# The last gate's sums traced behind the first expert group's products, and that group's gather taken apart between them

## The chip, the cores and the metric

The kernel runs on one core of a Trainium2 chip. The metric is the device time of one execution in microseconds. An engine is named as the profile names it: PE is TensorE, DVE is VectorE, ACT is ScalarE, POOL is GpSimd, and SP is the engine whose queue issues nearly all loads.

## What is computed

Two decoder layers over 256 tokens of width 1024, each a mixer followed by a mixture of 16 experts, of which every token uses two. Each layer takes shift, scale and gate vectors from a conditioning vector c. Cut to what matters here:

```
for layer in range(2):
    shift_m, scale_m, gate_m, shift_f, scale_f, gate_f = split(silu(c) @ ada_w[layer] + ada_b[layer], 6)
    x = x + gate_m * mixer(rmsnorm(x) * (1 + scale_m) + shift_m)
    h = rmsnorm(x) * (1 + scale_f) + shift_f
    group, two experts, weights w = route(sigmoid(h @ router_w) + router_b)
    y = sum over the two experts: w_e * ((silu(h @ w_gate[e]) * (h @ w_up[e])) @ w_down[e])
    x = x + gate_f * y
return rmsnorm(x)
```

The last gate of a layer, gate_f (number 5 of the six vectors), multiplies the experts' rows at the very end of an expert group.

## The kernel before

All weights, 4 bytes an element, stream from HBM through 15 slots of 1 MB (ten tiles "slot" and five "room"). One queue, SP's, issues the loads in the order of use, and a load waits there until its slot is free; everything behind it waits too. The instructions of each engine are put in order by a planner: it takes at each moment, by its own costs, the ready instruction that was traced first (a block under high_priority(-60) counts as traced some 60 instructions later), and it fills idle time with anything that is ready.

An expert stage (function moe) runs so in each layer:

- Router: transposes and products of X (L989, L992), sigmoid, then a long chain of small DVE operations that picks two experts for each token and numbers each expert's tokens (M, pos, route).
- fill(12) at L1056, under high_priority(-60), makes the last gate. ada_part (L327) multiplies the 4 MB of its weights by silu(c) in two parts (L340: matmuls of 32 columns into a bank with the tag "tp"). The partial sums go to a tile "adac", copied by ACT (L347) and added by DVE (L349). ada_end (L301) then sums over partitions: for each half of the gate one product with HALF (L307) into a tp bank and one addition on DVE (L309) into GATE[5]. There are two tp banks and two adac tiles.
- picked and gather (L1199, L1067) bring the tokens of group 0 together. pick (L1064) makes one-hot rows, and for each of the eight 128-feature pieces k four matmuls (L1073) select tokens out of the normalized x, held as a high and a low part. ACT (L1075, odd k) or DVE (L1077, even k) then applies scale and shift on the way from the tp bank to XG.
- places (L1384) sorts 13 of the experts by their number of tokens, on DVE (L1393 to L1406, with two adac tiles). Its result ex_p (L1405) holds the sorted expert numbers, and SP must read it before it can issue the loads of experts that aren't fixed.
- Then the loop over seven groups of 128 gathered rows. hidden() issues a group's gate and up loads and runs gate_up (L1103): eight steps k of gate products and eight of up products (L1091), 16 steps in a row, each with two 64-column matmuls. slots() makes the matrices that bring rows back to tokens (by_slot, L1135 and L1137), turn() transposes the hidden values (L1125), and rows() of the group before runs its down products and multiplies by the gate (L1162). The gather for groups 1 and 2 follows group 0 and for groups 3 to 6 later ones.

Groups 0 and 1 are special in their weights: group 0 has the fixed experts 14 and 15, so its eight loads (L1192) are issued long before the routing, and of group 1 one expert is fixed, with three of its loads (L1254) also ahead. These 11 MB and the gate's 4 MB fill all 15 slots. Slots come free when L340 is through with the gate's weights, and after that only as the products of group 0 are done.

Of the kernel before, what the change touches and what calls it, by code (L numbers as in the profile page):

```python
# [107 lines left out]
def trunk(ctx, tc, ins, out):  # L108
# [192 lines left out]
    def ada_end(layer, v, n, t):  # L301


        if n == 1:
            for half in range(2):
                b = bank("tp", [P, 512])
                last[0] = mm(b, HALF[:, half:half + 1].to_broadcast([P, P]), t, start=True, stop=True)  # L307
                sl = slice(half * 512, half * 512 + 512)
                vec.tensor_tensor(GATE[v][:, sl], GATE[v][:, sl], b, ALU.add)  # L309
            return  # L310
        b = bank("tp", [64, 8, 4])
        for k in range(8):
            last[0] = mm(b[:, k, :], t[:, 64 * k:64 * k + 64], ident[:, 0:128:32], start=True, stop=True)
        for i in range(2):
            o = MOD[layer, v + i]
            for half in range(2):
                sl = slice(64 * half, 64 * half + 64)
                vec.tensor_tensor(o[sl], b[:, :, 2 * i + half], ADC[sl, layer, v + i, :], ALU.add)
            if i:
                vec.scalar_tensor_tensor(o, o, 1.0, NRM[:, (v // 3) * 2 + layer, :], ALU.add, ALU.mult)  # L320

    def ada_tile():
        return wk.tile([P, 512], F32, tag="adac", name="adac")

    fills, sums, last = [], [], [None]

    def ada_part(layer, v, n, j, W):  # L327


        if j == 0:  # L330
            if n == 1:
                GATE[v] = big.tile([P, D], F32, name="GATE", tag="GATE")
                pool.dma_start(GATE[v], ins["ada_b"][layer:layer + 1, v * D:(v + 1) * D].to_broadcast([P, D]))
            sums.append(ada_tile())
        t = sums[0]
        b = bank("tp", [P, 512])
        for i in range(2):
            for g in range(4):
                k = 2 * j + i if n == 2 else 4 * j + 2 * i + g // 2
                last[0] = mm(b[32 * g:32 * g + 32], csil[:, k, :], W[i][:, g, :], start=i == 0, stop=i == 1)  # L340
            if i == 0:
                yield
        o, i = t, b
        if n == 2:
            o, i = t.rearrange("p (k m) -> p m k", k=8), b.rearrange("p (m k) -> p m k", k=8)
        if j == 0:
            act.copy(o, i)  # L347
        else:
            vec.tensor_tensor(o, o, i, ALU.add)  # L349
        if j == 2 * n - 1:  # L350
            yield
            ada_end(layer, v, n, sums.pop())

    def fill(n=1):
        for _ in range(n):
            if fills:
                at = fills.pop(0)
                W = first.pop(0) if first else ada_load(*at)
                for _ in ada_part(*at, W):
                    pass  # L360
# [613 lines left out]
    def moe(cp, wk, layer, norm, end):  # L974
# [77 lines left out]
        vec.tensor_reduce(ws, Wt, AX.X, ALU.add)  # L1052
        vec.reciprocal(ws, ws)
        vec.tensor_tensor(Wt, Wt, ws.unsqueeze(2).to_broadcast([P, 2, 16]), ALU.mult)
        with tc.high_priority(-60):
            fill(12)  # L1056
        gate = GATE[5]

        def pick(o, at, m):
# [4 lines left out]
                vec.tensor_tensor(o[:, t].rearrange("p (e s) -> p e s", e=n), iota,  # L1064
                                  at[:, t].unsqueeze(2).to_broadcast([P, n, m]), ALU.is_equal)

        def gather(XG, n, o):  # L1067

            for k in range(8):
                b = bank("tp", [P, n])  # L1070
                for t in range(2):
                    for i in range(2):
                        mm(b, xk[i][:, t, k, :], o[:, t, 0:n], start=t == i == 0, stop=t == i == 1)  # L1073
                if k % 2:
                    act.activation(XG[:, k, :], b, AF.Identity, bias=sh[:, k:k + 1], scale=fa[:, k:k + 1])  # L1075
                else:
                    vec.tensor_scalar(XG[:, k, :], b, fa[:, k:k + 1], sh[:, k:k + 1], ALU.mult, ALU.add)  # L1077
# [22 lines left out]
            at = [a for a, n in enumerate(ns) for _ in range(n)]  # L1100
            return [(at[j], slice(BLOCK * j, BLOCK * j + BLOCK)) for j in reversed(range(4))]

        def gate_up(XG, c0, parts, Wg, Wu):  # L1103

            out = []
            for W, tag in ((Wg, "mm"), (Wu, "sc")):
                b = bank(tag, [P, 512])
                put = in_line()
                for k in range(8):
                    for a, at in parts:  # L1110
                        put(b[at], XG[:, k, c0 + at.start:c0 + at.stop], W[a][k], start=k == 0, stop=k == 7)
                out.append(b)
                flush()
            g, u = out
            hid = wk.tile([P, 512], F32, tag="hid", name="hid", bufs=1)
            hq = wk.tile([P, 512], F32, tag="hq", name="hq", bufs=1)
            act.activation(hid, g, AF.Silu)
            vec.tensor_tensor(by_k(hq, 4), features(u, 4), features(hid, 4), ALU.mult)  # L1118
            return hq
# [79 lines left out]
        def picked(groups, pos):  # L1199

            o = pick_tile()
            places, at = [x for g in groups for x in GROUPS[g]], 0
            while places:
                p0, m = places[0]
                n = 1
                while n < len(places) and places[n] == (p0 + n, m):
                    n += 1
                pick(o[:, :, at:at + n * m * BLOCK], pos[:, :, p0:p0 + n], m * BLOCK)
                at += n * m * BLOCK
                places = places[n:]  # L1210
            return o, at

        def gathered(o, n):
            XG = hp.tile([P, 8, n], F32, tag="HT", name="XG")
            gather(XG, n, o)
            return o, XG

        class Group:
# [19 lines left out]
            def hidden(self):  # L1238
                names = ("moe_w_gate", "moe_w_up")
                if self.first:  # L1240
                    W = [load_both(nm, self.p0) for nm in names]
                elif self.mixed:
                    W = self.load_mixed(*names)
                else:
                    W = [load_experts(nm, self.es, 8, fine=self.last and nm == names[1]) for nm in names]
                self.hid = gate_up(self.XG, self.c0, self.parts, *W)

            def load_mixed(self, gate_, up):

# [238 lines left out]
                        go(i + 1)  # L1488
            go(0)

        o, XG = gathered(*picked([0], route[:, 0:2]))
        places()
        for h in range(2):
            vec.tensor_scalar(OT_x[:, h], ident.unsqueeze(1).to_broadcast([P, 2, P]), 0.0, None, ALU.mult)
# [2 lines left out]
        for i in range(len(GROUPS)):  # L1497
            p = Group(i, o, XG, 128 * (i > 0 and i % 2 == 0))
            if i == 3:
                flush()  # L1500
                rest()
            if p.last:
                end.load()
            p.hidden()
            if before is not None:
                before.rows()
            p.slots()
            p.turn()
            if i % 2 == 0 and i < 5:
                o, XG = gathered(*then)  # L1510
            elif i < 5:
                then = picked([i + 2, i + 3], placed[:, 0:2])
            if i == 0:
                rounds()
            flush()
            before = p
# [296 lines left out]
```

## Time and profile before

| | |
|---|---|
| median of 3 runs | 831.33 us (828.41 to 831.84) |
| the profiled execution | 828.97 us, its span 827.3 us |
| PE busy | 730.9 us (88%) |
| DVE busy | 379.0 us (46%) |
| ACT busy | 233.7 us (28%) |
| mean transfer rate | 352 GB/s |

All times of the trace are microseconds from the start of the span. The busy share of PE is an average over stages with different limits, so the stages have to be looked at one by one. A matmul of fp32 is two instructions in the trace, and neighbours in different columns of the array run at the same time. PEclk is the TensorE clock that was granted, as a part of 2.4 GHz.

### The profile page before, as it was taken

What the parts mean: (1) busy time and instruction counts of PE and PEld (TensorE: products, weight loads), DVE (VectorE), ACT (ScalarE), POOL (GpSimd) and SP (SyncE); (2) the same over time, 40 slices, a digit from 0 to 9 for tenths busy, and PEclk for the clock granted to TensorE, in tenths of its full rate; (3) what the DMA queues carried; (4) which work ended last, traced back from release to release, by engine and by line L of the source; (5) the groups of instructions that cost most, each with busy time, mean ns of one, the idle gap of its engine ahead of it and who ended that gap; (6) DMA issues with size and microseconds to landing.
All of it is one profiled execution on the core that took longest, in us unless ns stands there. A gap on an engine that the chain in (4) does not pass through costs nothing. (4 is left out here: it accounts for less than half of the span.)

```text
span 827.3 us, 12080 instructions
## 1 busy us (share of the span) xinstructions
PE 730.9 (88%) x4435; PEld 376.0 (45%) x4435; DVE 379.0 (46%) x1099; ACT 233.7 (28%) x565; POOL 101.0 (12%) x94
## 2 busy tenths in 40 slices
PE   4599999999799997899887899969899988899886
PEld 2298765557433342234222568547443332233223
DVE  2585777777841240312305754885931230322214
ACT  2264555545411110001012455544310110011012
POOL 1020211132200000000001223353100000000001
PEclk9899999999799998999999999998799998999998
DMA  9999878598399999999999987747399999999992
GB/s 355 339 372 418 316 255 256 221 419 321 131 426 374 426 427 424 426 426 427 427 426 414 374 338 210 279 172 279 117 426 377 427 426 423 426 425 428 422 414 91
DMA packets 68457, 291.15 MB, mean 352 GB/s; under 512 B 9174, under 2 KB 23202, under 8 KB 42530
## 3 DMA queue, kind: packets, MB, share of 16 engines
q1 hardware_dynamic: 64048, 283.53, 86.0%
q0 software_dynamic: 1152, 4.21, 1.3%
q10 hardware_dynamic: 3186, 2.51, 0.9%
q8 instruction: 39, 0.64, 0.3%
q14 instruction: 32, 0.26, 0.1%
HBM read 289.16 MB, written 1.06 MB: 351 GB/s over the span
## 5 line engine op out<-in xcount | busy, mean ns | idle before, releaser
L1091 PE MATMUL mm<-slot,XG 128*32 128x512 f32 (+1 forms) x464 | 107.6, 643 | 12.3 <-DMA slot<-in_moe_w_down_dram 6.3
L1091 PE MATMUL o<-slot,hT 128*32 128x512 f32 (+2 forms) x480 | 88.6, 589 | 2.5 <-DMA slot<-in_moe_w_down_dram 2.5
L1118 DVE TENSOR_TENSOR hq<-sc,hid 128x512 f32<-128x512 f32 x14 | 14.7, 1049 | 151.5 <-PE sc L1091 151.5
L514 ACT CAST hl<-slot 128x512 fp32r<-128x512 f32 (+2 forms) x112 | 60.9, 557 | 72.3 <-PE mm L531 41.8
L471 POOL TENSOR_TENSOR hl<-slot,hl 128x512 fp32r<-128x512 f32 x40 | 52.8, 1323 | 158.8 <-ACT hl L514 145.2
L1091 PE MATMUL sc<-slot,XG 128*32 128x512 f32 (+1 forms) x344 | 72.1, 593 | 0.0
L1091 PE MATMUL sc<-room,XG 128*32 128x512 f32 (+1 forms) x296 | 60.7, 593 | 1.2 <-DMA room<-in_moe_w_up_dram 1.2
L1091 PEld LDWEIGHTS mm<-slot,XG 128*32 128x32 f32 (+1 forms) x464 | 27.7, 129 | 69.3 <-issue 67.3
L529 PE MATMUL mm<-HH,hl 128*128 128x256 f32 x176 | 54.2, 310 | 4.7 <-ACT HH L503 4.7
L1162 DVE SCALAR_TENSOR_TENSOR adac<-o,w,GATE 128x512 f32<-128x512 f32 (+1 forms) x29 | 21.2, 732 | 79.0 <-PE o L1091 77.7
L1144 ACT CAST yg<-adac 128x512 fp32r<-128x512 f32 (+1 forms) x28 | 17.1, 612 | 137.9 <-DVE adac L1162 137.9
L1091 PE MATMUL mm<-room,XG 128*32 128x512 f32 (+1 forms) x176 | 52.8, 678 | 0.0
L531 PE MATMUL mm<-HH,hl 128*128 128x256 f32 x176 | 50.0, 286 | 0.8 <-DVE hl L471 0.8
L530 PE MATMUL mm<-HH,hl 128*128 128x256 f32 x176 | 50.2, 287 | 0.0
L471 DVE TENSOR_TENSOR hl<-slot,hl 128x512 fp32r<-128x512 f32 (+2 forms) x72 | 43.3, 623 | 13.5 <-ACT hl L514 13.2
L1091 PE MATMUL o<-room,hT 128*64 128x512 f32 (+2 forms) x176 | 47.4, 577 | 2.2 <-DMA room<-in_moe_w_down_dram 2.0
L340 PE MATMUL tp<-slot,csil 128*32 128x512 f32 x344 | 45.5, 611 | 3.3 <-DMA slot<-in_ada_w_dram 3.1
L1151 PE MATMUL tp<-yg,OT 128*128 128x512 f32 (+1 forms) x112 | 38.1, 441 | 11.1 <-DVE X L1152 5.2
L1073 PE MATMUL tp<-pick,XH 128*128 128x256 f32 (+1 forms) x128 | 39.8, 333 | 8.1 <-DVE XG L1077 4.7
L1152 DVE TENSOR_TENSOR X<-X,tp 128x512 f32<-128x512 f32 (+1 forms) x56 | 36.1, 674 | 17.4 <-PE tp L1151 17.1
L1075 ACT ACTIVATE XG<-tp,mod,mod 128x256 f32<-128x256 f32 (+1 forms) x32 | 17.2, 538 | 94.9 <-PE tp L1073 94.9
L1091 PEld LDWEIGHTS o<-slot,hT 128*32 128x32 f32 (+1 forms) x480 | 24.9, 119 | 40.8 <-issue 34.2
(372 smaller groups left out, 1272.6 us busy)
## 6 DMA issues: line engine op xcount, KB each, us to landing
slot<-in_moe_w_gate_dram SPq DMA_DIRECT2D x48, 1024.0 KB, 13.4
slot<-in_ada_w_dram SPq DMA_DIRECT2D x43, 1024.0 KB, 10.2
slot<-in_moe_w_down_dram SPq DMA_DIRECT2D x42, 1024.0 KB, 19.4
slot<-in_moe_w_up_dram SPq DMA_DIRECT2D x35, 1024.0 KB, 14.4
room<-in_moe_w_up_dram SPq DMA_DIRECT2D x27, 1024.0 KB, 10.1
room<-in_moe_w_down_dram SPq DMA_DIRECT2D x18, 1024.0 KB, 15.3
room<-in_moe_w_gate_dram SPq DMA_DIRECT2D x16, 1024.0 KB, 12.2
slot<-in_ev_w_in_dram SPq DMA_DIRECT2D x8, 1024.0 KB, 8.3
```

Of the source, the lines that this page charges most:

```text
L340: last[0] = mm(b[32 * g:32 * g + 32], csil[:, k, :], W[i][:, g, :], start=i == 0, stop=i == 1)
L471: return eng.tensor_tensor(lo, v, hi.bitcast(F32), ALU.subtract)
L514: act.copy(hi, src)
L529: mm(o, a[0], b[0], start=start, stop=False, skip_group_check=True)
L530: mm(o, a[0], b[1], start=False, stop=False, skip_group_check=True)
L531: mm(o, a[1], b[0], start=False, stop=stop, skip_group_check=True)
L1073: mm(b, xk[i][:, t, k, :], o[:, t, 0:n], start=t == i == 0, stop=t == i == 1)
L1075: act.activation(XG[:, k, :], b, AF.Identity, bias=sh[:, k:k + 1], scale=fa[:, k:k + 1])
L1091: last[0] = mm(*args, **kw)
L1151: mm(cb, OT[:, t, :], x, start=i == 0, stop=i == 1)
L1152: vec.tensor_tensor(X[:, t, sl], X[:, t, sl], cb, ALU.add)
L1162: vec.scalar_tensor_tensor(v, y, w, gate[:, sl], ALU.mult, ALU.mult)
```

## The change

Three things are done, in both layers. The sum of the last gate gets another home, the first half of a "yg" tile instead of an "adac" tile, and its end (ada_end: two L307, two L309) is put on a list and traced only behind hidden() of group 0. The gather of group 0 is no longer traced as a whole ahead of places(); gate_up of group 0 traces it itself, three pieces ahead of its first step and one piece ahead of each of the next five steps. And all eight of its pieces are evacuated by ACT. The other gathers stay as they were.

```
-            sums.append(ada_tile())
+            sums.append(homes[-1] if homes else ada_tile())
...
         if j == 2 * n - 1:
             yield
-            ada_end(layer, v, n, sums.pop())
+            t = sums.pop()
+            if homes:
+                ends.append(lambda: ada_end(layer, v, n, t))
+            else:
+                ada_end(layer, v, n, t)
...
+        homes.append(wk.tile([P, 2, 512], F32R, tag="yg", name="yg")[:, 0, :].bitcast(F32))
         with tc.high_priority(-60):
             fill(12)
+        homes.pop()
...
-        def gather(XG, n, o):
+        def gather(XG, n, o, ks=range(8), alone=False):
-            for k in range(8):
+            for k in ks:
...
-                if k % 2:
+                if alone or k % 2:
                     act.activation(XG[:, k, :], b, AF.Identity, bias=sh[:, k:k + 1], scale=fa[:, k:k + 1])
...
-        def gate_up(XG, c0, parts, Wg, Wu):
-            out = []
+        def gate_up(XG, c0, parts, Wg, Wu, o=None):
+            out, ks = [], list(range(8))
             for W, tag in ((Wg, "mm"), (Wu, "sc")):
                 b = bank(tag, [P, 512])
                 put = in_line()
                 for k in range(8):
+                    if o is not None and ks:
+                        n = 1 if k else 3
+                        gather(XG, 128, o, ks[:n], True)
+                        ks = ks[n:]
                     for a, at in parts:
...
-                self.hid = gate_up(self.XG, self.c0, self.parts, *W)
+                self.hid = gate_up(self.XG, self.c0, self.parts, *W, self.o if self.first else None)
...
-        o, XG = gathered(*picked([0], route[:, 0:2]))
+        o, _ = picked([0], route[:, 0:2])
+        XG = hp.tile([P, 8, 128], F32, tag="HT", name="XG")
         places()
...
             p.hidden()
+            while ends:
+                ends.pop()()
             if before is not None:
                 before.rows()
```

## Rows read from the trace of the kernel before

**Rows 1.** The page's line of transfer rates, the span in 40 equal slices.
```profile
GB/s 355 339 372 418 316 255 256 221 419 321 131 426 374 426 427 424 426 426 427 427 426 414 374 338 210 279 172 279 117 426 377 427 426 423 426 425 428 422 414 91
```

**Rows 2.** Table by stage: stretch, length, busy time by engine (instructions), PEclk, DMA share, GB/s.
```profile
211.20:224.20 13.00, 8.71 (x49) 4.71 (x41) 12.27 (x45) 3.61 (x6) 1.86 (x1) 0.86 0.00 1
253.80:262.00 8.20, 8.20 (x42) 2.77 (x40) 0.00 (x0) 0.60 (x1) 0.00 (x0) 1.00 0.88 302
...
578.60:593.40 14.80, 11.11 (x63) 5.01 (x62) 13.48 (x52) 5.98 (x8) 4.21 (x2) 0.85 0.00 2
623.00:632.00 9.00, 9.00 (x44) 3.02 (x42) 0.00 (x0) 0.60 (x1) 0.00 (x0) 1.00 0.91 312
```

**Rows 3.** Timeline of SP's queue, loads issued: start, length, line, operation, tile and source.
```profile
223.34 0.96 SPq L1254 DMA_DIRECT2D room<-in_moe_w_gate_dram  x2
...
241.06 2.05 SPq L1178 DMA_DIRECT2D slot<-in_moe_w_gate_dram  x2
...
254.39 0.33 SPq L1178 DMA_DIRECT2D slot<-in_moe_w_gate_dram  x1
257.82 0.33 SPq L1178 DMA_DIRECT2D slot<-in_moe_w_gate_dram  x1
...
626.84 0.33 SPq L1178 DMA_DIRECT2D slot<-in_moe_w_gate_dram  x1
```

**Rows 4.** Table by stage, columns as in Rows 2, inside the dip of layer 0.
```profile
254.30:256.50 2.20, 2.20 (x14) 0.76 (x12) 0.00 (x0) 0.00 (x0) 0.00 (x0) 1.00 0.63 160
...
258.50:260.10 1.60, 1.60 (x10) 0.56 (x8) 0.00 (x0) 0.00 (x0) 0.00 (x0) 1.00 0.86 184
```

**Rows 5.** Timeline of PE from routing to the products' end; idle time and releaser in brackets.
```profile
217.97 2.05 PE L307 MATMUL tp<-adac,HALF 128*128 128x512 f32 x2
219.80 0.48 PE L1073 MATMUL tp<-pick,XH 128*128 128x128 f32 x1
...
239.13 3.60 PE L1091 MATMUL sc<-slot,XG 128*64 128x512 f32 x16
...
589.35 0.33 PE L1073 MATMUL tp<-pick,XH 128*128 128x128 f32 x1 [0.77 <-DVE GATE L309]
...
609.86 1.88 PE L1091 MATMUL sc<-slot,XG 128*64 128x512 f32 x8
```

**Rows 6.** Timelines of DVE and ACT in layer 0, sorting and gather.
```profile
218.99 0.17 DVE L1406 COPY placed<-route 128x18 f32<-128x18 f32 x1
219.07 0.68 DVE L309 TENSOR_TENSOR GATE<-GATE,tp 128x512 f32<-128x512 f32 x1
...
220.90 0.40 DVE L1077 TENSOR_SCALAR XG<-tp,mod,mod 128x128 f32<-128x128 f32 x1
...
222.32 0.16 DVE L1405 CAST ex_p<-placed 1x13 int32<-1x13 f32 x1
...
226.71 0.32 DVE L1403 TENSOR_REDUCE placed<-adac 128x13 f32<-128x169 f32 x1
...
221.50 0.46 ACT L1075 ACTIVATE XG<-tp,mod,mod 128x128 f32<-128x128 f32 x1 [7.58 <-PE tp L1073]
```

**Rows 7.** Table by stage, PE alone: stretch, length, PE busy (instructions), PEclk, DMA share, GB/s.
```profile
224.00:230.40 6.40, 5.76 (x20) 0.50 0.97 360
...
244.00:256.00 12.00, 11.80 (x64) 1.00 0.97 390
```

**Rows 8.** Timeline of PE, the second gather between group 1's gate products.
```profile
248.59 0.64 PE L1091 MATMUL mm<-slot,XG 128*64 128x512 f32 x1
...
249.60 0.39 PE L1073 MATMUL tp<-pick,XH 128*128 128x256 f32 x1
...
250.75 0.64 PE L1091 MATMUL mm<-slot,XG 128*64 128x512 f32 x1
```

**Rows 9.** The chain of work that ended last, in order of time: a later group.
```profile
692.62 0.37 PE tp L1135 x2
...
693.33 3.57 PE mm L1091 x32
```

More of the change, by code (lines that the diff above doesn't have):

```diff
@@ L323, in ada_tile @@
         return wk.tile([P, 512], F32, tag="adac", name="adac")
-    fills, sums, last = [], [], [None]
+    fills, sums, last, homes, ends = [], [], [None], [], []
     def ada_part(layer, v, n, j, W):
```

## The prediction, made before the changed kernel was run

> **What bounds the kernel now.** I began with the transfer rate, since almost all the kernel does is to stream weights: the page's line of GB/s over 40 slices [rows 1]. Two slices fall to 131 and 117, the eleventh and the twenty-ninth. They are the routing of layer 0 and of layer 1, where the change acts. Behind either the rate stands at 424 to 427 for some ten slices, so the expert stages run at the pace of the weights, and what a faster routing is worth is the transfer time that it gives back, not PE time. A table by stage [rows 2] shows each of them as a stop and a dip. The stop is 13.0 us at 1 GB/s in layer 0 and 14.8 us at 2 GB/s in layer 1. The dip follows some 30 us later: 8.2 us at 302 GB/s, and 9.0 us at 312.
>
> The list of what SP issues tells why the transfers stop and dip [rows 3]. The first load that waits for a sorted expert number goes out at 223.34 us, right after DVE has written ex_p (222.32) [rows 6]; that ends the stop. Twelve loads of 1 MB are issued by 243.1 us. The thirteenth waits for a slot until 254.39, and the next two until 257.82; what frees these slots are products (L1091) of group 1. A fine table [rows 4] shows the price: the rate is 160 GB/s from 254.3 to 256.5, and 184 from 258.5 to 260.1, so 2.1 to 2.3 us pass from such an issue to full flow. In the dips 8.2 x (1 - 302/426) = 2.4 us are lost in layer 0 and 9.0 x (1 - 312/426) = 2.4 us in layer 1.
>
> Two moments therefore matter in each layer. One is when DVE writes ex_p. The other is how early TensorE (PE) gets through group 0's gate and up products, for every later slot is freed that much earlier. Between routing and products stands the gather: in layer 0 from 219.80 on, and the products end at 239.13 + 3.60 = 242.73; in layer 1 from 589.35, with the end at 609.86 + 1.88 = 611.74 [rows 5].
>
> **The change, part by part.** *The gate's sums.* The two products L307 and the two additions L309 are traced later, with nothing else changed in them. The instruction order is made by a planner, and I expect it to leave them where they are. It fills idle time with whatever is ready: in another group the two transposes of L1135, traced behind all of that group's gate and up products, run ahead of its second half [rows 9]; on DVE L1406, traced last in places(), runs ahead of L309 [rows 6]. The second L307 runs at 217.97, when the gather still waits for its one-hot rows; the sum that it reads is ready then in either kernel, and nothing more urgent is. So PE's queue up to the first piece, and the wait of that piece for L309 (layer 1's row names it [rows 5]), stay: cost and gain 0. If the sums do move, that is a rival, below. The new home of the sum (a yg tile) adds no instruction, and no yg is wanted before group 0's rows.
>
> *Evacuations.* Four pieces go from DVE (0.40 us each) to ACT (0.46 us) [rows 6]. One of the four DVE operations, at 220.90, stands in the chain that leads to ex_p; without it ex_p comes about 0.2 us earlier in each layer. On ACT eight pieces make 3.7 us on an engine with nothing else to do there. The third piece needs the bank of the first: emptied by ACT at 221.36 where DVE had it at 221.30, so 0.06 us later. The Trainium skill (page "Trainium Architecture — The Big Picture", section "The five engines, in one table") speaks against this part: ScalarE isn't for simple arithmetic, VectorE being up to three times as fast per element. The row shows 0.46 against 0.40 for these very shapes, so the measurement decides; by the page the third piece would come some 0.7 us later, and the gain worked out below would be 3.3 us instead of 4.3 (an estimate).
>
> *Pieces between products.* Now the first product needs three pieces, not eight. In layer 0 the third piece is through at about 221.9, 2.1 us after the gather's start; in layer 1 the first piece is 0.35 us shorter, as its first matmul takes 0.33 us instead of 0.48 [rows 5], so 1.75 us after its start, at 591.1. What follows is priced by the nearest rows: the second gather, which already runs interleaved with group 1's gate products [rows 8]. There one step of products takes 249.60 - 248.59 = 1.01 us, and eight matmuls of two pieces 250.75 - 249.60 = 1.15 us; four fewer at 0.12 leave 0.67 for one piece. Without a switch the products need 3.60/8 = 0.43 us a pair, 0.86 a step [rows 5]. So five steps with a piece cost 5 x 1.65 = 8.3 us, eleven without one 9.5, and the first switch 0.2: 17.9 us in all. The end comes at 239.8 and 609.0, which is 2.9 and 2.7 us earlier. The bounds are from these rows too: without the price of switching (4 x 0.12 + 0.86 a step) the lead is 4.6; with the half clock of the next paragraph it is about nothing. I take the second gather's price, for it is the same kind of work in the same order.
>
> *The clock.* In layer 0 the granted clock is 0.50 (1.2 GHz) for 6.4 us from the gather's second half on, although PE counts as busy 5.76 us of it; in the stretch of the interleaved second gather it is 1.00 (2.4 GHz) [rows 7]. The interleaved order of the first gather is like the second, so I take 1.00 after the third piece.
>
> **The sum.** In layer 0 the first dip goes whole: with a lead of 2.9 the thirteenth load is issued at 251.5, 2.6 us before the flow would end at 254.1. That load then ends at 254.1 + 2.4 = 256.5, and the next two, at full flow at 260.1 before, have it at 257.2: 0.7 us of gap remain, at 184 GB/s, so 0.4 us lost. Gain 2.4 - 0.4 + 0.2 = 2.2 us. In layer 1, where the second issue is at 626.84 [rows 3] and full flow some 2.3 us later, the gap is 0.9 and the loss 0.5: gain 2.4 - 0.5 + 0.2 = 2.1 us. Behind each dip the transfers run full to the stage's end, so both gains reach the end: 4.3 us. The profiled execution lasted 828.97 us (span 827.3 and 1.7 outside it) and would come to 824.7. It lies 2.4 below the median of the runs; from the median 831.33 I get 827.0.
>
> **The rivals.** *The clock stays low.* If interleaving doesn't hold 1.00, the 6.4 us at half speed are worth 3.2 at full; the short matmuls lose less than the long ones, so I put the loss of lead at 2.6, which leaves 0.3 in layer 0 and next to none in layer 1. For it: PE's work in the gather is short matmuls that wait for their weights; against it the row of the second gather. Time: 831.33 - 0.5 = 830.8.
>
> *The sums do move.* Then ex_p gains up to 1.4 us more, as the two L309 of 0.68 us leave its chain, and the gather starts 0.7 us earlier, by the one that it waits for. But PE then has nothing to do ahead of the gather. Behind the products the two L307 take about 1 us each (2.05 at the half clock [rows 5]) and hold both tp banks until two L309 are done, which sets back L1135 and the turn of group 0 by about 1.5 us, and the gather begins at the half clock, which costs 1 us or so. The lead falls to about 0.8 and 1.3, and with slots as the limit that is the gain: 829.2. The page "TensorE: Matmul & The Clock Gate" of the Trainium skill (section "Part 1: The HAM clock gate") says that throttled is the default and activity releases it; by it the gather would begin at the low clock, and the trace shows 0.48 us for the first matmul behind the idle time.
>
> *Slower: the additions are late.* L307 takes both tp banks early as now, but L309 is now less urgent than everything in places(). If the planner no longer puts the two additions into DVE's gaps, the first piece waits for them until places() is through (the last L1403 ends at 227.03) and one L309 is done: 227.7 instead of 219.8 [rows 6]. The lead is 2.9 - 7.9 = -5.0 a layer, and 841 us the time. It decides when the first piece starts later than 222.7. Against it: L1406 got its place between two links of that chain though it is the least urgent of places(), so the gaps are there for L309 too.
>
> **How the numbers follow.** Chances: forecast 0.57, clock low 0.13, sums moved 0.15, slower rival 0.10, another order further on by the planner with a loss 0.05. A measurement can tell about 0.5% (4.2 us) from no change. The forecast lies at that edge: 0.43 of its 0.57 go to faster, the rest to the same; clock low is the same, the moved sums nearly so (0.02 faster); the last two are slower. That makes 0.45 faster, 0.40 the same, 0.15 slower. The range goes from the full dips and 0.2 in both layers (5.2 us) with the runs' own 2.9 us below their median, 823, to the clock's rival with half a microsecond of scatter, 831.5; below and above it I leave 0.2.
>
> **What would show it.** Right: L307 and L309 ahead of the first piece; a first product 2 to 2.2 us behind it; a clock of 1.00 where it was 0.50; group 0's end 2.7 to 2.9 us nearer to the gather's start; a dip of under 1 us lost. Wrong: a product step with a piece of well over 1.65 us, a first piece that waits past 222.7, a dip as deep as before although PE leads, or a stop that got shorter by more than 0.3 us.

## The result, and the profile after

The changed kernel takes 835.04 us (median of 20 runs, 829.77 to 839.55) against 829.97 for the kernel before on the same chips (20 runs, 827.90 to 834.04). The ratio is 1.0057, with an interval of 1.0042 to 1.0072: slower by 5 us, where 4 us less had been forecast. All ratios in this text leave out runs that lie over 1.5% above the fastest of their kernel, and the profiles of e_inter and e_dup are of such runs.

The profiled execution lasted 836.81 us (span 835.1). Its PE timeline in layer 0 answers [rows 5]; the columns are start, length, engine, line, operation, tiles, count, and in brackets the idle time ahead with what ended it. Lines are those of the changed kernel: L1080 is the gather's matmul, L1098 a product.

```profile
212.29 2.36 PE L340 MATMUL tp<-slot,csil 128*32 128x512 f32 x16
217.87 0.17 PE L1045 MATMUL sc<-M,TRIB 128*128 128x16 bf16 x1 [3.21 <-DVE M L1042]
...
219.04 0.30 PE L1080 MATMUL tp<-pick,XH 128*128 128x128 f32 x1 [0.90 <-DVE pick L1071]
...
221.26 1.98 PE L1098 MATMUL mm<-slot,XG 128*64 128x512 f32 x4
223.17 0.48 PE L1080 MATMUL tp<-pick,XH 128*128 128x128 f32 x1
...
224.22 1.98 PE L1098 MATMUL mm<-slot,XG 128*64 128x512 f32 x4
...
241.03 3.60 PE L1098 MATMUL sc<-slot,XG 128*64 128x512 f32 x16
244.57 1.98 PE L307 MATMUL tp<-yg,HALF 128*128 128x512 f32 x4
246.47 0.44 PE L1146 MATMUL tp<-K,pick 128*128 128x128 f32 x2
...
247.91 0.39 PE L1080 MATMUL tp<-pick,XH 128*128 128x256 f32 x1
```

In the kernel before, the first of the two L307 stood there, behind an idle time too:

```profile
216.49 1.50 PE L307 MATMUL tp<-adac,HALF 128*128 128x512 f32 x2 [3.87 <-DVE adac L349]
```

Three things are to be seen. No L307 stands ahead of the gather any more: PE is idle for 3.21 us and again for 0.90, where the two L307 kept it busy from 216.49 up to the gather. They now run from 244.57, behind all products. A step of products with a piece takes 224.22 - 221.26 = 2.96 us, not 1.65. And the products end at 244.63 where they ended at 242.73, although the first product came at 221.26 instead of 226.86.

The table by stage of the same execution (stretch, length, busy time of PE, its weight loads, DVE, ACT, POOL, then PEclk, DMA share, GB/s) answers [rows 2, 4, 7].

```profile
212.00:220.00 8.00, 3.89 (x33) 1.73 (x25) 7.69 (x31) 2.55 (x5) 1.47 (x1) 0.92 1.02 429
220.00:224.00 4.00, 3.90 (x14) 2.06 (x12) 3.83 (x17) 1.07 (x3) 0.00 (x0) 0.51 0.66 205
224.00:232.00 8.00, 8.00 (x22) 2.84 (x21) 6.76 (x38) 1.37 (x3) 0.00 (x0) 0.50 1.01 421
232.00:236.00 4.00, 4.00 (x20) 2.20 (x20) 0.00 (x0) 0.92 (x2) 0.00 (x0) 0.79 1.01 426
...
252.00:256.00 4.00, 4.00 (x23) 2.08 (x22) 1.09 (x2) 1.04 (x2) 0.00 (x0) 1.00 0.42 178
256.00:260.00 4.00, 4.00 (x20) 1.35 (x20) 0.00 (x0) 0.56 (x1) 0.00 (x0) 1.00 0.25 33
260.00:264.00 4.00, 4.00 (x22) 1.41 (x20) 0.00 (x0) 0.60 (x1) 0.00 (x0) 1.00 0.93 313
```

PE's clock is 0.50 to 0.51, its lower level of 1.2 GHz, from 220 to 232 and rises only behind that; before it was low for 6.4 us from the gather's second half on [rows 7]. In layer 0 the gather still begins at 1.00 (0.30 us for its first matmul) and the clock falls 1.0 us later; in layer 1 it begins at 0.50 (0.44 us). And the dip is three times as deep: 4 x (1 - 178/426) + 4 x (1 - 33/426) + 4 x (1 - 313/426) = 7.1 us of transfer are lost, where 2.4 were. In layer 1 the rates of the four stretches of 4 us from 624 on are 371, 10, 246 and 328 GB/s, which makes 7.0. The stop did get shorter, since ex_p is written at 221.06 instead of 222.32, but in layer 0 that is 1.3 us against 4.7.

### The profile page after: what moved, and what is told of

It reads as the page before. It is cut to its first block, busy times and chain, and to the rows that moved or that the text cites. A ratio compares the mean times of both kernels' runs of the same rounds, so it can differ in the third digit from the quotient of the medians.

```text
span 835.1 us, 12081 instructions
## 1 busy us (share of the span) xinstructions
PE 742.5 (89%) x4435; PEld 380.8 (46%) x4435; DVE 376.1 (45%) x1091; ACT 237.4 (28%) x573; POOL 100.9 (12%) x94
## 4 chain that ended last, share of the span: by engine, by line
PE 32%; DMA 20%; DVE 6%; ACT 2%; issue 1%; SPq 0%; DVEq 0%; ACTq 0%
PE mm L1098 7%; DMA slot<-in_moe_w_down_dram 6%; DMA room<-in_moe_w_down_dram 5%; PE sc L1098 5%; DMA room<-in_moe_w_up_dram 5%; PE o L1098 5%; DMA slot<-in_moe_w_up_dram 2%; DMA slot<-in_moe_w_gate_dram 2%; PE tp L1080 2%; PE mm L533 1%; PE mm L534 1%; PE mm L535 1%; PE tp L1162 1%; PE tp L340 1%; PE tp L628 1%
## 5 line engine op out<-in xcount | busy, mean ns | idle before, releaser
L1098 PE MATMUL mm<-slot,XG 128*32 128x512 f32 (+1 forms) x464 | 112.8, 653 | 12.3 <-PEq L1497 6.4
L1098 PE MATMUL o<-slot,hT 128*32 128x512 f32 (+2 forms) x480 | 89.0, 597 | 2.7 <-DMA slot<-in_moe_w_down_dram 2.7
L1098 PE MATMUL sc<-slot,XG 128*32 128x512 f32 (+1 forms) x344 | 72.1, 593 | 0.0
L1098 PE MATMUL sc<-room,XG 128*32 128x512 f32 (+1 forms) x296 | 60.7, 593 | 0.0
L1098 PEld LDWEIGHTS mm<-slot,XG 128*32 128x32 f32 (+1 forms) x464 | 26.9, 129 | 62.5 <-issue 59.4
L1098 PE MATMUL o<-room,hT 128*64 128x512 f32 (+2 forms) x176 | 49.1, 598 | 4.3 <-DMA room<-in_moe_w_down_dram 4.3
L1098 PE MATMUL mm<-room,XG 128*32 128x512 f32 (+1 forms) x176 | 52.0, 679 | 0.0
L1082 ACT ACTIVATE XG<-tp,mod,mod 128x256 f32<-128x256 f32 (+1 forms) x40 | 20.9, 522 | 104.9 <-PE tp L1080 104.9
L340 PE MATMUL tp<-slot,csil 128*32 128x512 f32 x344 | 48.0, 640 | 2.4 <-DMA slot<-in_ada_w_dram 2.1
L475 DVE TENSOR_TENSOR hl<-slot,hl 128x512 fp32r<-128x512 f32 (+2 forms) x72 | 41.6, 599 | 17.7 <-ACT hl L518 17.5
L1080 PE MATMUL tp<-pick,XH 128*128 128x256 f32 (+1 forms) x128 | 41.4, 344 | 7.1 <-DVE XG L1084 2.8
L1098 PEld LDWEIGHTS o<-slot,hT 128*32 128x32 f32 (+1 forms) x480 | 24.9, 120 | 41.3 <-issue 35.4
```

Of the source, the lines that this page charges most:

```text
L475: return eng.tensor_tensor(lo, v, hi.bitcast(F32), ALU.subtract)
L1098: last[0] = mm(*args, **kw)
```

## The experiments

Two theories stood against each other at first. A: the loss comes from the moved sums, which leave PE idle ahead of the gather (low clock) and stand behind the products. B: the interleave itself is what is slow. Both turned out to hold a half of it. The first four runs take the change apart.

**e_inter**, the interleave alone. The list of ends and the new home of the sum are undone:

```
-            if homes:
-                ends.append(lambda: ada_end(layer, v, n, t))
-            else:
-                ada_end(layer, v, n, t)
+            ada_end(layer, v, n, t)
```

> The interleave alone: all eight pieces on ACT and placed between the products, but the last gate's sums (two L307, two L309) traced in their old place. Theory A (the loss comes from moving the sums: PE has nothing to do ahead of the gather, so its clock is low, and two L307 stand behind the products): here PE's queue ahead of the gather is that of before, the gather starts at 1.00, a step with a piece takes about 1.65 us, group 0's products end 2 to 3 us nearer to the gather's start, each dip loses under 1 us, and the time is 0.994 to 0.997 of before. Theory B (interleaving itself is what lowers the clock): the clock falls to 0.50 at the third piece and stays there through the steps of 2.95 us, and the time is 1.000 to 1.004 of before.

Measured: 832.98 us, but from 823.46 to 843.84 in twelve runs; ratio 0.9997 (0.9967 to 1.0028). Neither theory had expected such a width. With all twelve runs the mean is 832.43, 1.0035 of before. Three runs lie at 823.46 to 824.41 with a mean granted clock of 0.961 to 0.967, as the forecast had it; the longest have 0.904 to 0.950. In the profile (841.38 us) PE comes to the gather at the half clock in both layers, and all five steps with a piece take 2.95 us. The kernel before also comes to it at the half clock in layer 0 (0.50 from 218 to 220), so the 1.00 that A expected there was misread from it. So the interleave reaches the forecast at times, and the sums in their old place don't ensure it.

**e_defer**, the move of the sums alone:

```
-                self.hid = gate_up(self.XG, self.c0, self.parts, *W, self.o if self.first else None)
+                self.hid = gate_up(self.XG, self.c0, self.parts, *W)
...
-        o, _ = picked([0], route[:, 0:2])
-        XG = hp.tile([P, 8, 128], F32, tag="HT", name="XG")
+        o, XG = gathered(*picked([0], route[:, 0:2]))
```

> The move of the sums alone: L307 and L309 traced behind the first group's products, the gather whole, alternating between DVE and ACT, and ahead of places() as before. Theory A: L307 lands behind the products, PE is idle ahead of the gather, the gather runs at 0.50 and the first products too; the stop is some 1.5 us shorter in each layer, but group 0's products end 1 to 3 us later in relation to the gather's start and the turn another 2 us later; time 1.003 to 1.008 of before, about that of the changed kernel. Theory B: without the interleave the clock is as before, the stop is 1.5 us shorter in each layer, 2 us are added behind the products, and the time is 0.998 to 1.001 of before.

Measured: 833.57 us (830.52 to 835.34), ratio 1.0042 (1.0022 to 1.0061), in A's range. The PE timeline of layer 0, columns as above:

```profile
219.00 0.44 PE L1080 MATMUL tp<-pick,XH 128*128 128x128 f32 x1 [0.89 <-DVE pick L1071]
...
226.12 7.22 PE L1098 MATMUL mm<-slot,XG 128*64 128x512 f32 x24
...
238.32 3.60 PE L1098 MATMUL sc<-slot,XG 128*64 128x512 f32 x16
241.85 1.98 PE L307 MATMUL tp<-yg,HALF 128*128 128x512 f32 x4
243.75 0.44 PE L1146 MATMUL tp<-K,pick 128*128 128x128 f32 x2
```

But A's reason fails here. The gather does run at the half clock from its start, and yet from its first piece to the first product 7.12 us pass (7.06 before) and to the end of the products 22.92 (22.93 before, [rows 5]): at the full clock the whole gather waits for evacuations (in the kernel before for 0.42 and 0.64 us, released by XG), at the half clock PE is busy all through it, and both take the same time. In either kernel the clock then rises within the block of products (at 229.9 here, at 230.7 before). What is left is 0.8 us gained at the start and 1.9 us of L307 behind the products: L1146 comes 1.1 us later than its counterpart (243.75 against 242.66). The stop is 1.1 us shorter, too (the load behind ex_p at 222.22, 223.34 before [rows 3]), and that gave nothing. In layer 1 the gather starts 1.9 us later than before (591.23 against 589.35), for which the runs give no cause; so a part of the 4.3 us by which the profile is longer stays unexplained.

**e_dup**, the changed kernel with copies of the two L307 ahead of the gather that nobody reads:

```
                 ends.append(lambda: ada_end(layer, v, n, t))
+                for half in range(2):
+                    mm(bank("o", [P, 512]), HALF[:, half:half + 1].to_broadcast([P, P]), t, start=True, stop=True)
```

> The changed kernel with two more matmuls in each layer: copies of the two L307, into a bank of another tag, whose result nobody reads. They stand in PE's queue exactly where the L307 stood before; the sums themselves stay behind the products, and L309 stays there too. It adds work and takes nothing away. Theory A: the copies bring PE's clock at the start of the gather back to what it was before (1.00 for the first 4 us or more), the steps get shorter than 2.95 us, and the time is 0.996 to 1.000 of before, although work was added. Theory B: the clock falls as in the changed kernel (0.50 for some 13 us), and the time is 1.005 to 1.008 of before. If the clock comes back and the time doesn't, the 2 us of sums behind the products are the cause.

Measured: 831.51 us (826.56 to 839.65), ratio 1.0019 (1.0000 to 1.0038). Work was added and the kernel became faster than the changed one, which only the clock explains among the two theories; the mean granted clocks of its runs are 0.950 to 0.964, those of the changed kernel 0.939 to 0.958. But the copies don't ensure it: in the profiled execution, the longest of the twelve, they run at the half clock themselves (2.07 us for two instructions), and three steps take 2.95 us in either layer.

**e_nosum**, the changed kernel without the last gate's end (no L307, no L309):

```
-            if homes:
-                ends.append(lambda: ada_end(layer, v, n, t))
-            else:
+            if not homes:
                 ada_end(layer, v, n, t)
```

> The changed kernel without the last gate's two L307 and two L309 in either layer (this work is left out: that gate lacks its product and holds its bias alone). PE's queue up to the end of group 0's products is that of the changed kernel. Theory A with the clock as the larger part: the clock stays at 0.50 for some 13 us, only the 2 us behind the products go in each layer, and the time is 1.000 to 1.003 of before. Rival C (what costs is the 2 us of sums behind the products, the clock costs nothing that matters): the time is 0.995 to 0.998 of before, as the stop's 1.7 us and the interleave's lead are then kept.

Measured: 834.09 us (831.60 to 836.46, seven runs), ratio 1.0062 (1.0039 to 1.0085). Rival C is out. Theory A's number was too low as well: the 2 us a layer should have shown and didn't. The profile tells why a mean says little here. In layer 0 the clock rises during the second step; in layer 1 the gather begins at 1.00 (first matmul 0.30 us), the clock falls 0.9 us later, and all five steps with a piece take 2.95 us.

From here the theory was another: interleaved steps keep the clock that they meet. At 1.00 a step takes 1.60 us and the clock stays; at 0.50 it takes 2.95 and the clock tends to stay as well. Over all profiles of this text with the interleave, the clock stayed at 1.00 to the end of the products in each of the eleven layers whose first step began there; in the nine whose first step began at 0.50 it stayed low for between one step and all five. Which of the two it is should then depend on what PE did ahead. The next runs set that.

**e_obank**, the changed kernel with the banks of the two L307 from another tag:

```
-                b = bank("tp", [P, 512])
+                b = bank("o" if late_ else "tp", [P, 512])
```

> The changed kernel, with the two L307 of the moved sums writing to banks of the tag o instead of tp; everything is traced where the changed kernel traces it. Theory on the order (banks of one tag are handed out in the order of tracing, so L307 could not be put ahead of the gather's eight tp banks): the planner now puts both L307 back to where they stood before, one ahead of the routing products and one behind them, and the first piece waits for no L309. Theory on the time (group 0's products run at whichever clock the gather starts with, 1.60 us a step at 1.00 and 2.95 at 0.50, and the weights follow them one to one): as with the interleave alone, the time has two ends, some 823.5 where the clock is full and 838 or more where it is half; by the share of the two seen there the median is 0.996 to 1.003 of before. Rival (the place of the sums is what costs): all runs lie near 823 to 825, 0.993 of before.

The order in which the planner put PE's instructions, the changed kernel as minus and this one as plus, shows the first half at once:

```
 L340 MATMUL tp<-slot,csil 32x512 x8
+L307 MATMUL o<-yg,HALF 128x512
 L1045 LDWEIGHTS TRIB
...
 L1398 MATMUL sc<-M,TRIB 128x16
+L307 MATMUL o<-yg,HALF 128x512
 L1080 MATMUL tp<-pick,XH 128x128
...
 L1098 MATMUL sc<-slot,XG 64x512 x8
-L307 MATMUL tp<-yg,HALF 128x512 x2
 L1146 MATMUL tp<-K_105,pick 128x128 x2
```

With another tag both L307 go back to where they stood before, although they are traced as late as ever. That is what the theory on the order said: the banks of a tag go out in the order of tracing, and on tp the gather's eight come first.

Measured: 829.14 us (821.78 to 835.37), ratio 0.9972 (0.9939 to 1.0004); with all twelve runs the mean is 829.00, 0.9993 of before. The two ends are there: the two shortest runs have a mean granted clock of 0.971, the two longest 0.947 and 0.948. The profiled execution has both in one, layer 0 and then layer 1:

```profile
219.64 0.41 PE L1080 MATMUL tp<-pick,XH 128*128 128x128 f32 x1
...
220.20 1.98 PE L1098 MATMUL mm<-slot,XG 128*64 128x512 f32 x4
...
223.15 1.98 PE L1098 MATMUL mm<-slot,XG 128*64 128x512 f32 x4
...
592.31 0.28 PE L1080 MATMUL tp<-pick,XH 128*128 128x128 f32 x1
...
592.63 1.08 PE L1098 MATMUL mm<-slot,XG 128*64 128x512 f32 x4
...
594.23 1.08 PE L1098 MATMUL mm<-slot,XG 128*64 128x512 f32 x4
```

The same instructions in the same order take 2.95 us a step in layer 0, for three steps, and 1.60 in layer 1, where the clock rose just ahead of the third piece. From first piece to the products' end that is 25.3 us against 20.6.

**e_warm**, the changed kernel with matmuls that nobody reads in PE's idle time, the sums still behind the products:

```
+        def busy(n, w, after=None):
+            with tc.high_priority(-60):
+                for _ in range(n):
+                    with tc.issue_after(after) if after else nullcontext():
+                        mm(bank("o", [P, 256]), w.to_broadcast([P, P]), X[:, 0, 0:256], start=True, stop=True)
+        busy(3, pr[:, 0, 5:6])
+        busy(6, m2[:, 0:1])
+        busy(2, m2[:, 0:1], placed_.ins)
```

> The changed kernel with eleven matmuls more in each layer that nobody reads (128x256, into banks of the tag o): nine in PE's idle time ahead of the routing products and two between these and the first piece. The sums stay behind the products. Theory of the clock: PE is kept at 1.00 up to the gather, the steps with a piece take 1.60 us instead of 2.95, group 0's products end 6 to 7 us nearer to the gather's start than in the changed kernel's profile, and the time falls to 0.993 to 0.998 of before (the 2 us of the sums behind the products are still paid in each layer). Rival (something else than the clock sets the steps): the steps stay at 2.95 us and the time at 1.005 or above, as the added matmuls can only delay.

Measured: 826.38 us, eleven of the twelve runs between 823.78 and 829.35, the twelfth at 882.96 with a mean granted clock of 0.828; ratio 0.9964 (0.9948 to 0.9980). Eleven matmuls more a layer make the changed kernel 0.9% faster. The PE timeline of layer 0 (L1108 are the products), and PE alone from a table by stage:

```profile
218.28 0.30 PE L1090 MATMUL tp<-pick,XH 128*128 128x128 f32 x1
...
222.15 1.08 PE L1108 MATMUL mm<-slot,XG 128*64 128x512 f32 x4
...
223.75 1.08 PE L1108 MATMUL mm<-slot,XG 128*64 128x512 f32 x4
...
238.14 1.98 PE L307 MATMUL tp<-yg,HALF 128*128 128x512 f32 x4
```

```profile
212.00:240.00 28.00, 26.98 (x131) 1.00 0.96 393
```

The clock is 1.00 throughout. The steps take 1.60 us in both layers (but for the first, which holds one of the added matmuls and takes 2.09), and the products end 19.9 us behind the first piece (25.6 in the changed kernel). The rival is out.

**e_warmb**, seven such matmuls in the kernel before:

```
+        busy(3, pr[:, 0, 5:6])
+        busy(4, m2[:, 0:1])
```

> The kernel before, with seven such matmuls in PE's idle time ahead of the routing products; the gather whole and the sums in place. It prices the warm clock without the change. Theory of the clock: the whole gather runs at 1.00 at its start, as in the profile of before, or longer; what was at 0.50 behind it was 6.4 us, so 1 to 3 us a layer can be gained and the time is 0.993 to 0.998 of before. If the whole gather lowers the clock whatever stood ahead of it, the second half of it stays at 0.50 and the time is 0.999 to 1.001.

Measured: 829.92 us (827.76 to 831.99), ratio 1.0007 (0.9993 to 1.0020), the second of the two cases. PE alone, layer 0:

```profile
214.00:223.00 9.00, 8.28 (x47) 1.00 0.00 0
...
224.00:230.00 6.00, 5.71 (x21) 0.50 0.87 322
```

The gather starts at the full clock, and behind its middle the clock falls as it did before. A warm start alone is worth nothing with the whole gather, as e_defer had shown from the other side. What a clock that stays up through the whole gather would be worth, no run shows.

**e_obwarm**, e_obank with the same seven matmuls:

> The changed kernel with the two L307 on banks of the tag o and with the seven matmuls of the run on the kernel before in PE's idle time: the sums early, the clock kept up, the pieces between the products. Theory of the clock: all of the forecast's conditions hold, steps of 1.60 us, products that end 2.5 to 3.5 us earlier than in the kernel before, dips of under 1 us, and nearly all runs at 822 to 826, 0.991 to 0.995 of before. Rival (the clock falls during the interleave whatever went before): two ends again, 823 and 838, and a median of 0.997 to 1.003.

Measured: 825.00 us (821.51 to 827.59, six runs), ratio 0.9947 (0.9926 to 0.9968); all steps at 1.60 us. The clock wasn't kept up, though: it was 0.50 from 216 to 219 in layer 0 and from 585 to 588 in layer 1, and rose ahead of the first piece. In layer 0 four of the added matmuls waited for a DVE result (m2) and then ran until 218.9, so the routing products came 2 us late. The last three runs do without that: eight matmuls that need only pr.

```
+        busy(8)        # w = pr[:, 0, 5:6]
```

**e_iwarm** adds them to e_inter:

> The interleave alone (sums in their old place, on tp) with eight matmuls more in each layer that nobody reads, in PE's idle time ahead of the first L307, so that nothing stands between them and the routing products that waits. These are the forecast's own conditions: sums in place, interleave, full clock. If the forecast's sum holds under them, the time is 0.994 to 0.996 of before (4.3 us less is 0.9948) and the runs lie close together. Rival (the first piece's wait for L309 and the DVE's share of the chain eat the lead): 0.998 to 1.000.

Measured: 823.85 us (822.29 to 828.56, seven runs), ratio 0.9940 (0.9919 to 0.9962), so 5.0 us less than before: the forecast's sum under the forecast's conditions. The PE timeline of layer 0 (L1064 are the added matmuls), and the table by stage where the dips were:

```profile
210.71 3.72 PE L1064 MATMUL o<-X,prs 128*128 128x256 f32 x16
216.34 1.12 PE L307 MATMUL tp<-adac,HALF 128*128 128x512 f32 x2 [1.91 <-DVE adac L349]
...
219.00 0.33 PE L1082 MATMUL tp<-pick,XH 128*128 128x128 f32 x1 [0.47 <-DVE pick L1073]
...
221.01 1.08 PE L1100 MATMUL mm<-slot,XG 128*64 128x512 f32 x4
...
222.61 1.08 PE L1100 MATMUL mm<-slot,XG 128*64 128x512 f32 x4
...
235.08 3.60 PE L1100 MATMUL sc<-slot,XG 128*64 128x512 f32 x16
```

```profile
250.00:254.00 4.00, 4.00 (x21) 1.30 (x19) 0.00 (x0) 0.24 (x1) 0.00 (x0) 1.00 1.01 422
254.00:258.00 4.00, 4.00 (x22) 1.43 (x20) 0.00 (x0) 0.36 (x1) 0.00 (x0) 1.00 1.01 424
258.00:262.00 4.00, 4.00 (x22) 1.42 (x18) 1.06 (x1) 0.00 (x0) 0.00 (x0) 1.00 1.00 414
...
624.00:628.00 4.00, 4.00 (x21) 1.37 (x19) 0.00 (x0) 0.00 (x0) 0.00 (x0) 1.00 1.01 424
```

The products end 19.68 us behind the first piece, 3.25 earlier than before, and there is no dip left in either layer.

**e_best** adds them to e_obank:

> The changed kernel with the two L307 on banks of the tag o and the same eight matmuls. In the earlier run with seven matmuls four of them waited for a late DVE result and pushed the routing products of layer 0 back by 2 us; here none waits for it. Theory of the clock: routing products right behind M, steps of 1.60 us, nearly all runs at 820 to 825, 0.990 to 0.994 of before, and 0.001 to 0.003 better than the interleave with the sums on tp, whose first piece waits for L309. Rival (the place of the sums matters little once the clock is full): no difference between the two, 0.994 to 0.996 both.

Measured: 824.56 us (820.94 to 826.50, six runs), ratio 0.9935 (0.9910 to 0.9959). It can't be told from e_iwarm, so the rival holds: with a full clock it matters little on which banks the sums are, as long as they stand ahead of the gather. Behind the products they do cost time: in e_warm's profile the products of layer 0 end 0.4 us earlier than here (238.21 against 238.57), but its second gather starts 1.3 us later (241.49 against 240.19).

**e_alt** is e_best with the eight pieces emptied by DVE and ACT in turn:

```
-                        gather(XG, 128, o, ks[:n], True)
+                        gather(XG, 128, o, ks[:n])
```

> As the run before this one, but the eight pieces are emptied by DVE and ACT in turn, as in the kernel before. It prices the move of four evacuations to ACT. By the forecast's row (0.46 us against 0.40) and with the stop's end hidden behind the slots it is worth nothing: within 0.002 of the run with all eight on ACT, the third piece within 0.3 us. Rival (DVE, which is in the middle of the routing chain, serves pieces late): first products 0.5 to 1 us later and a time 0.001 to 0.003 higher.

Measured: 825.59 us (823.21 to 826.26, six runs), ratio 0.9946 (0.9928 to 0.9965). The first product comes 2.03 us behind the first piece instead of 1.78; the times can't be told apart.

**Seven profiles side by side.** For layer 0 of the profiled execution: the first piece, the third step of products, the products' end counted from the first piece, the start of the second gather, and what had been moved by 280 us (summed from a table of stretches of 10 us).

| kernel | first piece | step | products' end | second gather | MB by 280 us |
|---|---|---|---|---|---|
| before | 219.80 | (whole gather) | +22.93 | 244.36 | 91.67 |
| after | 219.04 | 2.95 | +25.59 | 247.91 | 90.13 |
| e_inter | 219.82 | 2.96 | +29.27 | 250.72 | 89.00 |
| e_defer | 219.00 | (whole gather) | +22.92 | 245.20 | 91.31 |
| e_nosum | 218.85 | 1.60 | +22.61 | 243.09 | 92.33 |
| e_warm | 218.28 | 1.60 | +19.93 | 241.49 | 92.82 |
| e_iwarm | 219.00 | 1.60 | +19.68 | 240.30 | 92.97 |

The last two columns belong together. From before to after the second gather comes 3.55 us later and 1.54 MB are missing, which is 3.6 us at the full flow of 0.426 MB a us; for e_inter it is 6.36 us and 2.67 MB (6.3 us), for e_warm 2.87 us earlier and 1.15 MB more (2.7 us). Here every microsecond by which the second gather comes later is a microsecond of transfer lost. It ends where the dip is gone: e_iwarm is another 1.2 us earlier than e_warm and has 0.15 MB more. Of the profiles that the table leaves out, e_obwarm departs from it: its second gather is 1.96 us earlier, but it has only 0.38 MB more (0.9 us), for its ex_p was written 1.6 us late and its stop lasted longer.

The lag also reaches the end. By 740 us the changed kernel has 3.54 MB less than the kernel before, which is 8.3 us, and its span is 7.8 us longer; for e_inter it is 12.4 us and 12.4, for e_iwarm 4.5 us more and a span 5.1 shorter.

## Why the prediction was wrong

**What bounds the kernel: right.** How early PE is through group 0 sets when the later slots come free, and that sets the time, one to one up to the point where the dip is gone, as the table shows. An earlier ex_p counts only once the slots come in time: in e_defer it came early and the bytes came late. (The "424 to 427 for some ten slices" passes over a slice of 374 and one of 377 [rows 1], which are the dips.)

**The sums stay where they are: wrong, and the first step that failed.** The argument was that the planner fills idle time with whatever is ready, whenever it was traced. It does, but an instruction that needs a bank of tp also needs its turn among the banks of that tag, and the gather's eight stood ahead of it. The row that I took for evidence [rows 9] showed an instruction that had the next bank of its tag anyway; L1406, the other one, needs none. e_obank shows that the tag alone decides. With the clock held at 1.00 (e_warm) the moved sums leave 0.9964, where the forecast had 0.9948 with them in place: by these two numbers this step is the smaller part of the error, 1.3 us.

**The rival of the moved sums: the place right, the price wrong.** It had named what happened (PE idle ahead of the gather, L307 behind the products, an earlier ex_p), and 1.90 us between 244.57 and 246.47 is what it said of L307. But it put the low clock at "1 us or so" and so came out 2 us faster than before. In layer 0 of the changed kernel the turn (L1146 for L1135) is 246.47 - 242.66 = 3.81 us late: -0.76 from the earlier first piece, +2.66 from the products, +1.90 from L307.

**The clock: wrong, and the larger error.** I took 1.00 for the interleaved first gather because the interleaved second gather has 1.00 [rows 7, 8]. But the second gather starts behind a long block of products at 1.00, and the first doesn't; the row showed that an interleave can keep a clock, not that it makes one. In layer 0 of the kernel before, the granted clock is 0.50 from 218 to 220, where the gather starts: the 2.05 us of L307 and the 0.48 us of the first matmul [rows 5] were signs of it. (The rival on the moved sums read the 0.48 us as an effect of idle time; in layer 1, where the first matmul does stand behind 0.77 us of it, it takes 0.33.) For the low clock I took over the 6.4 us of the kernel before. There it ended within the block of products behind the gather; in the interleave it went on, in layer 0 of e_inter from 216 to 240, and in layer 1 of e_nosum through all the steps with pieces. A step at 0.50 costs 2.95 - 1.60 = 1.35 us more; four of them (the changed kernel's layer 0) make 5.4 us, where the rival on the clock had 2.6 in all. Between the changed kernel (1.0057) and e_warm (0.9964), which holds the clock and leaves the sums behind the products, lie 7.7 us of the 9.0 between forecast (0.9948) and measurement. Nor did the low clock need the moved sums: e_inter has it with the sums in place. The rival on the clock was the upper end of the range (830.8), so the range was too low for the same reason.

The Trainium skill (page "TensorE: Matmul & The Clock Gate", section "Part 1: The HAM clock gate") says that the default is throttled and that activity releases it, and that the warm-up varies from run to run. The first statement would have spoken for a low start. The runs agree in part: behind idle time the gather begins at 0.50 in both layers of e_defer, but in layer 0 of the changed kernel at 1.00. They agree with the variation (821.78 to 835.37 us for one kernel, e_obank, at mean granted clocks of 0.971 to 0.947). With one row the first statement does not agree: from 224 to 232 the changed kernel's PE is busy 8.00 of 8.00 us, and its clock stays at 0.50.

**Evacuations: right.** All on ACT or in turn makes no difference in time that can be measured (e_alt). In the profiles ex_p is written 2.57 us behind the first piece with all on ACT (e_best) and 2.96 in turn (e_alt), where 0.2 us had been forecast.

**Pieces between products: right.** 1.65 us a step was forecast and 1.60 measured at the full clock; a lead of 2.9 us in layer 0 and 2.7 in layer 1, and 3.25 and 2.71 measured (e_iwarm).

**The sum: right under its conditions.** Forecast 4.3 us, measured 5.0 (3.2 to 6.7) with the sums in place and the clock held up. The dip went whole, where 0.4 and 0.5 us had been left to it.

**The rival on the late additions: not seen.** L309 didn't hold up the first piece in the changed kernel, whose piece waits for its one-hot rows alone.

What stays open: why e_nosum isn't faster than the changed kernel in the mean, though it has 2 us less behind the products in each layer. Its profile answers for one execution. It gains 1.5 us in layer 0 and loses about 4 in layer 1, where the clock was low, and it loses another 3.3 us from 695 to 710 us, where it moves 332 GB/s and the kernel before and the changed one 423 and 425. Ahead of that PE stood for 4 us without a cause that the profile names:

```profile
694.38 1.06 PE L1096 MATMUL mm<-slot,XG 128*32 128x512 f32 x1 [4.09 <-issue]
```

Whether its other six runs have this, no trace shows. And the 2 us themselves are measured only roughly: e_warm to e_best is 0.9964 to 0.9935, with intervals that overlap.

## What to carry to other kernels

Work that is moved out of PE's idle time can cost more than its own time: read the granted clock behind the gap, and price an interleave of short and long matmuls at both levels before pricing it at one. A lead in PE is real only if the clock that it is priced at is there at its start; a few matmuls that nobody reads can hold it up, as they did in every profile of e_warm, e_iwarm, e_best and e_alt; the two copies of e_dup, which had to wait for their operand, did not. And a planner that fills gaps is bound by the order in which buffers of a tag are handed out: an instruction traced late with a buffer of a busy tag stays late.

## What the runs showed of the hardware

Two things had not been expected. One is how self-keeping either clock level is in an interleave: the same sequence ran at 2.95 and at 1.60 us a step in one execution of e_obank, and adding eleven matmuls a layer to the changed kernel took it from 1.0057 to 0.9964 of before. The other is a side effect of the interleave on SP's in-order queue. In layer 0 of the changed kernel the planner put a load of group 0 that has to wait for a room ahead of five that needn't:

```profile
162.05 1.06 SPq L256 DMA_DIRECT2D room<-in_ada_w_dram  x2
180.31 0.37 SPq L1203 DMA_DIRECT2D room<-in_moe_w_gate_dram  x1
180.78 0.41 SPq L256 DMA_DIRECT2D slot<-in_ada_w_dram  x1
```

From 170 to 180 us the rate is 108 GB/s, where it was 420, and by 200 us 4.3 MB are missing. They were made up while the routing held the next loads (427 GB/s from 210 to 220 us, where it was 34): by 220 us the changed kernel has 68.7 MB and the kernel before 69.3, and by 240 us it is 0.5 MB ahead. All kernels here with the interleave have this order, the fastest too.
